# First modulation sums in halves of c, a first pass over two k tiles, `uhi` of the first tiles on ScalarE, and later gate-weight loads

## The chip, the cores and the metric

The kernel runs on one core of one Trainium2 chip. A core has a matrix engine, TensorE (PE in the rows below, with PEld for its weight loads), and VectorE (DVE), ScalarE (ACT), GpSimd (POOL) and SyncE (SP), each with its own instruction queue that is worked in order; they meet at semaphores. The metric is the device time of one execution in microseconds, as the median of several runs.

## The reference

Two layers of a decoder trunk work on x (256 tokens by 1024 channels) under a conditioning vector c of 1024. Each layer has three sub-layers: a SwiGLU channel mixer, a sequence mixer (recurrent in layer 0, attention in layer 1) and another channel mixer. All are modulated by c:

```python
c_act = jax.nn.silu(c)
for l in range(DEPTH):
    mod = c_act @ mod_w[l] + mod_b[l]
    sh1, sc1, g1, sh2, sc2, g2, sh3, sc3, g3 = jnp.split(mod, N_MOD, axis=-1)
    f = swiglu(modulate(x, sh1, sc1), ffn_in[l, 0], ffn_out[l, 0])
    x = deepnorm_residual(x, f, g1, ln_g[l, 0], ln_b[l, 0], 0.5)
    ...
```

`modulate(x, shift, scale)` is `x * (1 + scale) + shift`, and `swiglu(u, w_in, w_out)` is `(silu(u @ gate half) * (u @ up half)) @ w_out` with a hidden width of 2816, 22 tiles of 128. What matters here is the very first channel mixer: its input u needs shift and scale, and each of their 1024 values is a sum over 1024 products of c with a row of `mod_w`.

## The kernel before

**Layout.** Channels lie on the 128 partitions, in KD = 8 tiles, and the 256 tokens on the free axis. All weights are cut into tiles of 128x128 and stored in the order of their use; 16 tiles make a slab of 1 MB, `wst[s]`, and 170 slabs make up the whole plan. A second list of 72 slabs, `modw`, holds the modulation weights: each has two rows-of-`mod_w` tiles of 128x1024, in the first eight slabs the shift and the scale of one k tile.

**Precision.** A product is made of three matmuls (`mm3`, L413 to L422): the weights are split into `whi` (ACT, a rounding copy, L348) and `wlo` (DVE, the rest, L349), and u into `uhi` and `ulo`; hi times hi, lo times hi and hi times lo are added in PSUM. A slab is converted in two halves of 1024 columns, so it takes two `whi`, two `wlo` and 48 matmuls. Only slab 0 (k = 0 of the first pass) is taken as it came, with plain float32 matmuls (L417).

**Streams.** The class `Stream` (L303 on) issues the loads on SyncE, into a pool of six buffers `wraw` that weight slabs and modulation slabs share; `FIRST_MODS` (L227) says how many modulation slabs are to be asked for by each of the first twelve weight slabs, and the first eight also bring one tile of x with them (L388). `conv_to` converts slabs some halves ahead of their use. `reduce` (L392 to L401) makes one value per partition of a modulation tile: one DVE instruction that multiplies with `cact`, the activated c on every partition, sums, and starts from the bias column `mod_b`; a short read of the accumulator follows it.

**The first channel mixer.** The pairs of gate and up tiles are worked in passes, each over a group of eight pairs that fill the eight PSUM banks:

```python
a, b = range(GRP), range(GRP, 2 * GRP)
return [(a, range(KSPLIT)), (b, range(KD)), (a, range(KSPLIT, KD))]
```

With KSPLIT = 4, group a is taken over k = 0 to 3, its partial sums are copied out of PSUM by ACT (L761), group b runs over all eight k, and group a ends over k = 4 to 7, where the copies are added (L767). One k of one group is exactly one slab. Before a slab that uses a new k, `first_u(k)` (L515 to L533) makes u for it: two sums, `scp` = 1 + scale on DVE (L525), `ut` on ACT (L527), `uhi` on DVE (L531), `ulo` = `ut` - `uhi` on DVE (L532), and ax = ALPHA times x on ACT (L539).

**What sets the order.** The framework's scheduler lays the instructions out on each engine's queue, by the order in which the code asks for them and by priorities (`tc.high_priority`); `queue_behind` ties one instruction behind another without a semaphore. In the recurrent mixer of layer 0, each of eight gate-weight tiles `rgt` is loaded by a DMA that ACT issues (L865); three buffers are free from the start, so the first three issues stand at the head of ACT's queue. `shift_out` (L587 on) copies the first output tile of a sub-layer in ACT (L593) for a matmul with ones, whose result is subtracted from ax on POOL.

**The start.** c arrives, two matmuls with a row of ones spread it over the partitions (L453), ACT applies SiLU in two halves (`cact`, L442), and twelve matmuls with no use for their result (L459) follow on PE ahead of the first slab.

Of the kernel before, what the change touches and what calls it, by code (L numbers as in the profile page):

```python
# [21 lines left out]
P = 128  # L22
DM = 1024
# [8 lines left out]
NMOD = 9  # L32
# [3 lines left out]
MH, NOPE, ROPE, MV = 8, 128, 64, 128  # L36
QR, KVR = 256, 128
SLAB = 16
GRP = 8
KSPLIT = 4  # L40
GRPE = 4
EARLY = 1

# [180 lines left out]
    return out  # L224


FIRST_MODS = (1, 2, 3, 4, 4, 4, 5, 5, 6, 7, 8, 8)  # L227
SHARE = (13, 11, 18, 18, 0, 4)
SKIP = (12, 14, 6, 6, 3, 8)
ENDGAP = 1  # L230
# [4 lines left out]
def trunk_kernel(ctx: ExitStack, tc: tile.TileContext, xT, cvec, pos, wst, modw, colsd,  # L235
# [24 lines left out]
    def T(pl, shape, dt=F32, tag=None, **kw):  # L260
        return pl.tile(shape, dt, tag=tag, name=nm(tag), **kw)
# [41 lines left out]
    class Stream:  # L303
# [74 lines left out]
        def mods_to(self, n):  # L378
            while self.nmod < n:
                t = T(wraw, [P, 2, DM], tag="wraw")  # L380
                if self.nmod:
                    sync.dma_start(t, modw[self.nmod])
                else:
                    sync.dma_start(t[:, 0, :], modw[0, :, 0])
                    sync.dma_start(cols, colsd)
                    sync.dma_start(t[:, 1, :], modw[0, :, 1])
                if self.nmod < KD:
                    sync.dma_start(x0[:, self.nmod, :], xT[:, self.nmod, :])  # L388
                self.todo += [(2 * self.nmod + q, t[:, q, :], self.ndma) for q in range(2)]
                self.nmod += 1  # L390

        def reduce(self):  # L392
            i, t, _ = self.todo.pop(0)
            l, v, j = MODS[i]
            if (l, v) not in self.modcols:
                self.modcols[(l, v)] = T(const, [P, KD], tag=f"mod{l}_{v}")
            junk = T(wk, [P, DM], BF16, tag="junk", bufs=1)
            i = vec.tensor_tensor_reduce(junk, t, cact, 1.0, col("mod_b", (l * NMOD + v) * KD + j),  # L398
                                         MULT, ADD, self.modcols[(l, v)][:, j:j + 1])
            if self.behind is not None:  # L400
                queue_behind(i, self.behind)  # L401
# [48 lines left out]

    for i in range(2):
        ps = mmps()
        pe.matmul(ps, one_row, crow[:, i * 512:(i + 1) * 512], start=True, stop=True)  # L453
        ta(cact[:, i * 512:(i + 1) * 512], ps, AF.Silu)


    ps = mmps()
# [50 lines left out]
        ta(cosT, n, AF.Sin, scale=-1.0, bias=hp)  # L508


    scp0 = T(const, [P, KD], tag="scp0")
    W.dma_to(1)
    first_done = set()

    def first_u(k):  # L515
        if k in first_done:
            return
        first_done.add(k)

        W.mods_to(k + 1)  # L520
        while W.todo and W.todo[0][0] < 2 * k + 2:
            W.reduce()
        kk = slice(k, k + 1)
        sc0, sh0 = W.modcols[(0, SC)], W.modcols[(0, SH)]
        vec.tensor_scalar(scp0[:, kk], sc0[:, kk], 1.0, None, ADD)  # L525
        ut = T(wk, [P, SEQ], tag="ut")
        act.activation(ut, x0[:, k, :], AF.Identity, bias=sh0[:, kk], scale=scp0[:, kk])  # L527
        if k < RAWSLABS:
            u_raw[k] = ut
        else:  # L530
            vec.tensor_scalar(uhi[:, k, :], x0[:, k, :], scp0[:, kk], sh0[:, kk], MULT, ADD)  # L531
# [10 lines left out]
    class Boundary:  # L542
# [44 lines left out]
        def shift_out(self):  # L587


            y = self.y[:, 0, :]  # L590
            yr = T(wk, [P, SEQ], F32R, tag="shift", bufs=1)
            with tc.high_priority():
                act.activation(yr, y, AF.Copy)  # L593
            sp = axps()
            pe.matmul(sp[:, :SEQ], ones_r, yr, start=True, stop=True)
            shift = T(wk, [P, SEQ], tag="shift", bufs=1)
            with tc.high_priority():
                act.activation(shift, sp[:, :SEQ], AF.Copy)  # L598
                for j in range(1, KD):
                    pool.tensor_tensor(ax[:, j, :], ax[:, j, :], shift, SUB)  # L600
                vec.tensor_tensor(y, y, shift, SUB)
                ysq = T(wk, [P, SEQ], tag="ysq")
                act.activation(ysq, y, AF.Square)
                self.scaled(0)
            self.p0 = (y, ysq)
# [220 lines left out]
    def even(l, prev):  # L826
        with tc.tile_pool(name=nm("even"), bufs=1) as ep, tc.tile_pool(name=nm("ew"), bufs=2) as ew:
# [28 lines left out]
            def rglru(j0):  # L856
                rg1 = T(ep, [P, 2, RB, SEQ], tag="ya1")
                rg2 = T(ep, [P, 2, RB, SEQ], tag="ya2")
                xc, tz, pz, ww = rg1[:, 0], rg1[:, 1], rg2[:, 0], rg2[:, 1]
                for q in range(RB):  # L860
                    j = j0 + q
                    kk = slice(j, j + 1)
                    x = xc[:, q, :]
                    rgt = T(ew, [P, 2, P], tag="rgt", bufs=3)
                    act.dma_start(rgt, rgw[j])  # L865
                    act.activation(x, xa[:, j, hw:], AF.Identity, bias=col("conv_b", j),
                                   scale=col("conv_w", hw * KD + j))
# [484 lines left out]
```

## Time and profile before

| what | value |
|---|---|
| runs | 1031.18, 1032.38 and 1034.73 us; median 1032.38 |
| profiled execution | 1033.28 us, of which the span from the first instruction to the last is 1031.5 us |
| granted TensorE clock, mean | 0.992 |
| weights and the rest read from HBM | 256.18 MB, 249 GB/s over the span |
| `whi`, ACT, 128x1024 | 338 of 1056 ns |
| `wlo`, DVE, 128x1024 | 338 of 1228 ns |
| modulation sum, DVE, 128x1024 | 144 of 1294 ns |

The profile is one execution, recorded by the hardware. A row of the view in order of time gives the start, the length (both in us), the engine, the line, the operation, what it writes and reads, and in brackets how long the engine stood idle before it and what ended that. "x2" joins two equal instructions that follow each other; the next one can start a little before the end of the last, so two `wlo` of 1.23 take 2.36. A busy PE is not PE at its peak, since matmuls overlap: two that follow each other start 0.11 apart and are shown with 0.28 each.

### The profile page before, as it was taken

Reading aid. Unit: us, or ns where it says so; the run is one execution under the profiler, and the core shown is the slowest. Engines: PE = TensorE matmul, PEld = TensorE weight load, DVE = VectorE, ACT = ScalarE, POOL = GpSimd, SP = SyncE. Lnnn points to the kernel's source line nnn. Section 1 sums busy time; section 2 is a strip of 40 time slices with the busy share of each in tenths; the row PEclk is TensorE's granted clock in tenths of the full one; section 3 lists DMA queues with packets and bytes.
Section 4 is the critical chain, followed back from the end, with each engine's and each line's share of the span. In section 5 each row is a group of like instructions: output and inputs, shape, how many; then the busy total and the mean of one; then the engine's idle time right before and its main releaser. Section 6 shows DMA issues by size and latency. Waiting matters only on the chain.

```text
span 1031.5 us, 20651 instructions
## 1 busy us (share of the span) xinstructions
PE 1001.4 (97%) x8346; PEld 978.3 (95%) x8346; DVE 887.0 (86%) x1498; ACT 606.2 (59%) x1014; POOL 54.7 (5%) x70
## 2 busy tenths in 40 slices
PE   8999999999999989999999999999999999999995
PEld 6999999998989979999999999999999889999995
DVE  5889999798999789999897899999888799666664
ACT  3646664678886656645545674454568666545442
POOL 0000011000000020000030000003000200000200
PEclk9999999999999999999999999999999999999998
DMA  9998798655566924799976479987743236666411
GB/s 345 415 349 323 272 347 313 232 203 193 196 247 258 346 98 170 261 377 377 363 290 251 165 261 371 344 330 324 286 164 123 83 127 255 237 240 244 166 41 41
DMA packets 38578, 258.57 MB, mean 251 GB/s; under 512 B 4289, under 2 KB 6849, under 8 KB 7762
## 3 DMA queue, kind: packets, MB, share of 16 engines
q1 hardware_dynamic: 37330, 256.20, 66.3%
q8 instruction: 65, 1.06, 0.4%
q10 hardware_dynamic: 1152, 1.05, 0.3%
q14 instruction: 31, 0.25, 0.1%
HBM read 256.18 MB, written 1.05 MB: 249 GB/s over the span
## 4 chain that ended last, share of the span: by engine, by line
PE 82%; DVE 11%; ACT 3%; issue 2%; DMA 2%; POOL 0%; SPq 0%; ACTq 0%; DVEq 0%
PE mm L420 25%; PE mm L422 25%; PE mm L421 25%; DVE wlo L349 3%; DVE junk L398 2%; DMA rgt<-rgw 1%; DMA wraw<-modw 1%; PE mm L1022 1%; PE mm L1021 1%; PE mm L1023 1%; ACT whi L348 1%; PE ax L422 1%; PE ax L421 1%; PE ax L420 1%; DVE acc L618 0%
## 5 line engine op out<-in xcount | busy, mean ns | idle before, releaser
L349 DVE TENSOR_TENSOR wlo<-wraw,whi 128x1024 fp32r<-128x1024 f32 x338 | 412.1, 1228 | 76.4 <-ACT whi L348 75.5
L420 PE MATMUL mm<-uhi,whi 128*128 128x256 f32 x1660 | 458.3, 278 | 7.9 <-ACT whi L348 3.6
L421 PE MATMUL mm<-ulo,whi 128*128 128x256 f32 x1660 | 458.7, 277 | 0.5 <-DVE ulo L463 0.5
L422 PE MATMUL mm<-uhi,wlo 128*128 128x256 f32 x1660 | 456.4, 277 | 0.5 <-DVE wlo L349 0.5
L348 ACT ACTIVATE whi<-wraw 128x1024 fp32r<-128x1024 f32 x338 | 353.6, 1056 | 171.9 <-PE mm L421 139.0
L420 PEld LDWEIGHTS mm<-uhi,whi 128*128 128x128 f32 x1660 | 311.3, 188 | 9.9 <-ACT whi L348 4.4
L421 PEld LDWEIGHTS mm<-ulo,whi 128*128 128x128 f32 x1660 | 312.3, 188 | 1.0 <-DVE ulo L463 0.7
L422 PEld LDWEIGHTS mm<-uhi,wlo 128*128 128x128 f32 x1660 | 311.5, 188 | 0.8 <-DVE wlo L349 0.7
L422 PE MATMUL mm<-hhi,wlo 128*128 128x256 f32 x704 | 194.5, 276 | 0.8 <-DVE wlo L349 0.8
L421 PE MATMUL mm<-hlo,whi 128*128 128x256 f32 x704 | 194.3, 276 | 0.0
L420 PE MATMUL mm<-hhi,whi 128*128 128x256 f32 x704 | 194.3, 276 | 0.0
L398 DVE CUSTOM_DVE_ANT_0 junk<-wraw,cact,cols 128x1024 bf16<-128x1024 f32 x144 | 186.4, 1294 | 7.3 <-DMA wraw<-modw 6.7
L422 PEld LDWEIGHTS mm<-hhi,wlo 128*128 128x128 f32 x704 | 132.2, 188 | 1.0 <-DVE wlo L349 1.0
L420 PEld LDWEIGHTS mm<-hhi,whi 128*128 128x128 f32 x704 | 132.2, 188 | 0.0
L421 PEld LDWEIGHTS mm<-hlo,whi 128*128 128x128 f32 x704 | 132.2, 188 | 0.0
L600 POOL TENSOR_TENSOR ax<-ax,shift 128x256 f32<-128x256 f32 x42 | 47.9, 1173 | 840.8 <-ACT shift L598 667.2
L462 ACT ACTIVATE hhi<-h 128x256 fp32r<-128x256 f32 x88 | 35.7, 413 | 61.2 <-DVE h L731 60.9
L614 ACT ACTIVATE ysq<-yy 128x256 f32<-128x256 f32 x42 | 17.4, 414 | 60.8 <-DVE yy L610 58.8
L610 DVE SCALAR_TENSOR_TENSOR yy<-mm,gate,ax 128x256 f32<-128x256 f32 x48 | 22.9, 478 | 17.7 <-PE mm L422 16.5
L731 DVE SCALAR_TENSOR_TENSOR h<-mm,sg 128x256 f32<-128x256 f32 x75 | 30.8, 416 | 8.1 <-PE mm L422 8.1
L463 DVE TENSOR_TENSOR hlo<-h,hhi 128x256 fp32r<-128x256 f32 x88 | 35.8, 415 | 0.0
L442 ACT ACTIVATE sg<-mm 128x256 f32<-128x256 f32 x75 | 27.5, 367 | 4.2 <-PE mm L422 3.0
(296 smaller groups left out, 1103.4 us busy)
## 6 DMA issues: line engine op xcount, KB each, us to landing
wraw<-wst SPq DMA_DIRECT2D x169, 1024.0 KB, 5.2
wraw<-modw SPq DMA_DIRECT2D x71, 1024.0 KB, 7.1
wraw<-modw SPq DMA_DIRECT2D x2, 512.0 KB, 5.3
rgt<-rgw ACTq DMA_DIRECT2D x8, 128.0 KB, 4.6
yy<-xT SPq DMA_DIRECT2D x8, 128.0 KB, 9.2
wraw<-wst SPq DMA_DIRECT2D x2, 512.0 KB, 6.4
outT<-yy SPq DMA_DIRECT2D x3, 256.0 KB, 2.7
outT<-yy SPq DMA_DIRECT2D x2, 128.0 KB, 2.7
```

The lines of the kernel that those rows point to most:

```text
L348: act.activation(hi, raw, AF.Copy)
L349: i = vec.tensor_tensor(lo, raw, hi.bitcast(F32), SUB)
L398: i = vec.tensor_tensor_reduce(junk, t, cact, 1.0, col("mod_b", (l * NMOD + v) * KD + j), MULT, ADD, self.modcols[(l, v)][:, j:j + 1])
L420: pe.matmul(ps, hi, mh, start=start, stop=False, skip_group_check=shared)
L421: pe.matmul(ps, hi, ml, start=False, stop=False, skip_group_check=shared)
L422: pe.matmul(ps, lo, mh, start=False, stop=stop, skip_group_check=shared)
L442: i = act.activation(out, in_, func, **kw)
L462: act.activation(hi, src, AF.Copy)
L463: return vec.tensor_tensor(lo, src, hi.bitcast(F32), SUB)
L600: pool.tensor_tensor(ax[:, j, :], ax[:, j, :], shift, SUB)
L610: vec.scalar_tensor_tensor(y, ps, self.gate[:, f:f + 1], ax[:, f, :], MULT, ADD)
L731: vec.scalar_tensor_tensor(h, pu, bu, sg, ADD, MULT)
```

## The change

It has four parts.

1. The first modulation slab is loaded in two halves of c (columns 0 to 511 of both tiles, then the rest), not tile by tile. The first two sums are made in halves: `modh` takes the first half's sum, with the bias, and the second half starts from it. The 1 + of the scale moves into the bias column `scb`, made once, so `scp` is gone for all eight k.
2. KSPLIT is 2, so the first pass is over k = 0 and 1, group b runs over eight k as before, and group a ends over k = 2 to 7. `FIRST_MODS` follows: slabs 0 and 1 bring a modulation slab each, slab 2 none, slabs 3 to 8 one each.
3. `uhi` of k = 1 to 7 is made on ACT, ahead of `ut`.
4. The first three loads of `rgt` are queued behind the copy in the first `shift_out` (`mark`).

```diff
-KSPLIT = 4
+CH = DM // 2
+KSPLIT = 2
...
-FIRST_MODS = (1, 2, 3, 4, 4, 4, 5, 5, 6, 7, 8, 8)
+FIRST_MODS = (1, 2, 2, 3, 4, 5, 6, 7, 8, 8, 8, 8)
...
-                    sync.dma_start(t[:, 0, :], modw[0, :, 0])
+                    sync.dma_start(t[:, :, :CH], modw[0, :, :, :CH])
                     sync.dma_start(cols, colsd)
-                    sync.dma_start(t[:, 1, :], modw[0, :, 1])
+                    sync.dma_start(t[:, :, CH:], modw[0, :, :, CH:])
...
-            i = vec.tensor_tensor_reduce(junk, t, cact, 1.0, col("mod_b", (l * NMOD + v) * KD + j),
+            if i < 2:
+                if i == 0:
+                    for q in range(2):
+                        tq = self.first[:, q, :CH]
+                        lq, vq, jq = MODS[q]
+                        vec.tensor_tensor_reduce(junk[:, :CH], tq, cact[:, :CH], 1.0,
+                                                 mod_init(lq, vq, jq), MULT, ADD, modh[:, q:q + 1])
+                vec.tensor_tensor_reduce(junk[:, CH:], t[:, CH:], cact[:, CH:], 1.0, modh[:, i:i + 1],
+                                         MULT, ADD, self.modcols[(l, v)][:, j:j + 1])
+                return
+            i = vec.tensor_tensor_reduce(junk, t, cact, 1.0, mod_init(l, v, j),
...
+    def mod_init(l, v, j):
+        return scb[:, j:j + 1] if (l, v) == (0, SC) else col("mod_b", (l * NMOD + v) * KD + j)
...
+    vec.tensor_scalar(scb, col("mod_b", SC * KD, KD), 1.0, None, ADD)
...
-        sc0, sh0 = W.modcols[(0, SC)], W.modcols[(0, SH)]
-        vec.tensor_scalar(scp0[:, kk], sc0[:, kk], 1.0, None, ADD)
+        scp0, sh0 = W.modcols[(0, SC)], W.modcols[(0, SH)]
+        if k >= RAWSLABS:
+            act.activation(uhi[:, k, :], x0[:, k, :], AF.Identity, bias=sh0[:, kk], scale=scp0[:, kk])
         ut = T(wk, [P, SEQ], tag="ut")
         act.activation(ut, x0[:, k, :], AF.Identity, bias=sh0[:, kk], scale=scp0[:, kk])
...
-            vec.tensor_scalar(uhi[:, k, :], x0[:, k, :], scp0[:, kk], sh0[:, kk], MULT, ADD)
...
-                act.activation(yr, y, AF.Copy)
+                self.mark = act.activation(yr, y, AF.Copy)
...
-                    act.dma_start(rgt, rgw[j])
+                    i = act.dma_start(rgt, rgw[j])
+                    if j < 3:
+                        queue_behind(i, prev.mark)
```

The order of the instructions shows where this leads. On ACT, the first pass and what follows it stood before like this, from the `ut` of k = 2 to the first copy of a partial sum (names end in a buffer's number; `wraw` is a slab as loaded, `yy` holds x):

```order
L527 ACTIVATE ut_310<-yy_115,mod_0_41_167,scp_23_141 128x256
L348 ACTIVATE whi_213<-wraw_184 128x1024
L348 ACTIVATE whi_227<-wraw_184 128x1024
L539 ACTIVATE ax_138<-yy_115 128x256
L527 ACTIVATE ut_374<-yy_115,mod_0_41_167,scp_23_141 128x256
L348 ACTIVATE whi_249<-wraw_189 128x1024
L348 ACTIVATE whi_279<-wraw_189 128x1024
L761 ACTIVATE flat_88_440<-mm_159 128x512
L348 ACTIVATE whi_317<-wraw_191 128x1024
L348 ACTIVATE whi_345<-wraw_191 128x1024
```

After the change, ACT has from the copies of the last partial sums to the slab that follows k = 3:

```order
L783 ACTIVATE flat_76_311<-ax_168 128x512
L561 ACTIVATE ax_140<-yy_115 128x256
L548 ACTIVATE uhi_138<-yy_115,mod_0_42_169,mod_1_44_174 128x256
L550 ACTIVATE ut_459<-yy_115,mod_0_42_169,mod_1_44_174 128x256
L349 ACTIVATE whi_250<-wraw_189 128x1024
L349 ACTIVATE whi_282<-wraw_189 128x1024
L561 ACTIVATE ax_140<-yy_115 128x256
L548 ACTIVATE uhi_138<-yy_115,mod_0_42_169,mod_1_44_174 128x256
L550 ACTIVATE ut_526<-yy_115,mod_0_42_169,mod_1_44_174 128x256
L349 ACTIVATE whi_333<-wraw_194 128x1024
L349 ACTIVATE whi_365<-wraw_194 128x1024
```

The `uhi` and `ut` of k = 2 now stand ahead of the `whi` of slab 3, those of k = 3 ahead of slab 4, and so on; with k = 7 alone the two `whi` stand between `uhi` and `ut`.

On DVE, before, one k ended and the next slabs' `wlo` followed, with no sums between them for three slabs (`junk` is a sum's unused product; the row behind it reads the accumulator):

```order
L525 TENSOR_SCALAR scp_23_141<-mod_1_43_170 128x1
L531 TENSOR_SCALAR uhi_136<-yy_115,scp_23_141,mod_0_41_167 128x256
L532 TENSOR_TENSOR ulo_137<-ut_374,uhi_136 128x256
L349 TENSOR_TENSOR wlo_250<-wraw_189,whi_249 128x1024
L349 TENSOR_TENSOR wlo_280<-wraw_189,whi_279 128x1024
L349 TENSOR_TENSOR wlo_318<-wraw_191,whi_317 128x1024
L349 TENSOR_TENSOR wlo_346<-wraw_191,whi_345 128x1024
L349 TENSOR_TENSOR wlo_385<-wraw_207,whi_384 128x1024
L349 TENSOR_TENSOR wlo_413<-wraw_207,whi_412 128x1024
L398 ISA junk_467,mod_0_41_167<-wraw_244,cact_96,cols_97 128x1024
```

Now DVE has, from the second `wlo` of slab 2 on:

```order
L350 TENSOR_TENSOR wlo_231<-wraw_184,whi_230 128x1024
L413 ISA junk_254,mod_0_42_169<-wraw_186,cact_96,cols_97 128x1024
L413 ISA mod_0_42_169 128x1
L413 ISA junk_256,mod_1_44_174<-wraw_186,cact_96,scb_117 128x1024
L413 ISA mod_1_44_174 128x1
L554 TENSOR_TENSOR ulo_139<-ut_459,uhi_138 128x256
L350 TENSOR_TENSOR wlo_251<-wraw_189,whi_250 128x1024
L350 TENSOR_TENSOR wlo_283<-wraw_189,whi_282 128x1024
L413 ISA junk_337,mod_0_42_169<-wraw_191,cact_96,cols_97 128x1024
L413 ISA mod_0_42_169 128x1
L413 ISA junk_339,mod_1_44_174<-wraw_191,cact_96,scb_117 128x1024
L413 ISA mod_1_44_174 128x1
```

The same group of two sums, `ulo` and two `wlo` comes six times in a row, for k = 2 to 7 and slabs 3 to 8.

The third place is ACT around the first `shift_out`, where the copy of `yy` (L593 before) was followed by a `whi` and the copy of the shift; now three DMA issues stand between:

```order
L615 ACTIVATE shift_1965<-yy_1794 128x256
L887 DMA rgt_3143<-rgw 128x256
L887 DMA rgt_3159<-rgw 128x256
L887 DMA rgt_3175<-rgw 128x256
L349 ACTIVATE whi_1955<-wraw_1694 128x1024
L620 ACTIVATE shift_1969<-ax_1967 128x256
```

These are the three issues that stood ahead of everything but a table load and one copy at the head of ACT's queue.

More of the change, by code (lines that the diff above doesn't have):

```diff
@@ L383, in mods_to @@
                 else:
-                    sync.dma_start(t[:, 0, :], modw[0, :, 0])
+                    sync.dma_start(t[:, :, :CH], modw[0, :, :, :CH])
                     sync.dma_start(cols, colsd)
-                    sync.dma_start(t[:, 1, :], modw[0, :, 1])
+                    sync.dma_start(t[:, :, CH:], modw[0, :, :, CH:])
                 if self.nmod < KD:
                     sync.dma_start(x0[:, self.nmod, :], xT[:, self.nmod, :])
+                if self.nmod == 0:
+                    self.first = t
                 self.todo += [(2 * self.nmod + q, t[:, q, :], self.ndma) for q in range(2)]
@@ L410, in trunk_kernel @@
     x0 = T(main, [P, KD, SEQ], tag="yy")
+    modh = T(const, [P, 2], tag="modh")
+    scb = T(const, [P, KD], tag="scb")
+    def mod_init(l, v, j):
+        return scb[:, j:j + 1] if (l, v) == (0, SC) else col("mod_b", (l * NMOD + v) * KD + j)
     W = Stream()
@@ L452, in trunk_kernel @@
         ps = mmps()
-        pe.matmul(ps, one_row, crow[:, i * 512:(i + 1) * 512], start=True, stop=True)
-        ta(cact[:, i * 512:(i + 1) * 512], ps, AF.Silu)
+        pe.matmul(ps, one_row, crow[:, i * CH:(i + 1) * CH], start=True, stop=True)
+        ta(cact[:, i * CH:(i + 1) * CH], ps, AF.Silu)
     ps = mmps()
@@ L508, in rope_tables @@
         ta(cosT, n, AF.Sin, scale=-1.0, bias=hp)
-    scp0 = T(const, [P, KD], tag="scp0")
     W.dma_to(1)
+    vec.tensor_scalar(scb, col("mod_b", SC * KD, KD), 1.0, None, ADD)
     first_done = set()
```

## The prediction

> **What bounds the kernel now.** I read the page first, then the busy time by stretch, then who waited for whom on TensorE, then the three engines' instructions in order of time up to 70 us.
>
> ```profile
> span 1031.5 us, 20651 instructions
> PE 1001.4 (97%) x8346; PEld 978.3 (95%) x8346; DVE 887.0 (86%) x1498; ACT 606.2 (59%) x1014; POOL 54.7 (5%) x70
> PE mm L420 <- ACT whi L348: 3.6, 3, 1.6
> 19.40:26.16 6.76, 5.77 (x48) 5.57 (x48) 5.85 (x10) 2.91 (x5) 0.00 (x0) 1.00 1.02 418
> 26.16:32.91 6.75, 5.77 (x48) 5.57 (x48) 5.84 (x10) 2.80 (x5) 0.00 (x0) 1.00 1.01 421
> 64.90:124.00 59.10, 58.64 (x518) 58.44 (x516) 58.02 (x97) 37.14 (x63) 0.00 (x0) 1.00 0.78 292
> 124.00:163.30 39.30, 38.52 (x337) 38.32 (x337) 39.30 (x66) 20.02 (x27) 8.98 (x7) 1.00 0.89 340
> ```
>
> TensorE (PE) is busy for 97% of the span: a saving anywhere else counts only where it shortens a wait of PE. The changed instructions stand in the first 160 us, so I look for PE's waits there. The third row (wait, total, times, longest) gives three waits for `whi` between 10 and 70 us. The stretches (length, then busy time of PE, PEld, DVE, ACT, POOL, granted clock, DMA share, GB/s) show a slab of 48 matmuls taking 6.76 us twice, and VectorE (DVE) nearly full from 65 to 163 us. PE's own rows, in order of time:
>
> ```profile
> 6.03 4.37 PE L459 MATMUL mm<-ones_dm,ident 128*128 128x128 f32 x24
> 10.63 5.45 PE L417 MATMUL mm<-ut,wraw 128*128 128x256 f32 x24 [0.23 <-ACT ut L527]
> 19.41 0.38 PE L420 MATMUL mm<-uhi,whi 128*128 128x256 f32 x1 [1.60 <-ACT whi L348]
> 24.90 0.28 PE L422 MATMUL ax<-uhi,wlo 128*128 128x256 f32 x1
> 26.17 0.38 PE L420 MATMUL mm<-uhi,whi 128*128 128x256 f32 x1 [0.99 <-ACT whi L348]
> 32.92 0.38 PE L420 MATMUL mm<-uhi,whi 128*128 128x256 f32 x1 [0.99 <-ACT whi L348]
> 38.56 0.28 PE L420 MATMUL mm<-uhi,whi 128*128 128x256 f32 x1
> 66.03 0.28 PE L420 MATMUL mm<-uhi,whi 128*128 128x256 f32 x1
> 124.03 0.38 PE L422 MATMUL mm<-uhi,wlo 128*128 128x256 f32 x1 [0.49 <-DVE wlo L349]
> 163.40 0.38 PE L422 MATMUL mm<-hhi,wlo 128*128 128x256 f32 x1 [0.85 <-DVE wlo L349]
> ```
>
> I number slabs by the order of the plan: slab 0 is the raw one (L417), slab 1 starts at 19.41, slab 4 at 38.56 and slab 9 at 66.03. From 38.56 on PE does not wait for long: (66.03 - 38.56) / 5 = 5.49 us a slab. Slab 1, which starts cold, ends at 24.90 + 0.11, so 5.60 from its start. After that PE waits only twice, 0.49 and 0.85, both for DVE's `wlo`.
>
> **Why slabs 2 and 3 cost 6.76.** This is one turn, on DVE and then ACT:
>
> ```profile
> 24.20 0.08 DVE L398 DVE_READ_ACCUMULATOR2_ANT mod<- 128x1 f32 x1
> 24.31 0.15 DVE L525 TENSOR_SCALAR scp<-mod 128x1 f32<-128x1 f32 x1
> 24.50 0.41 DVE L531 TENSOR_SCALAR uhi<-yy,scp,mod 128x256 fp32r<-128x256 f32 x1
> 26.15 2.36 DVE L349 TENSOR_TENSOR wlo<-wraw,whi 128x1024 fp32r<-128x1024 f32 x2 [0.52 <-ACT whi L348]
> 28.42 1.28 DVE L398 CUSTOM_DVE_ANT_0 junk<-wraw,cact,cols 128x1024 bf16<-128x1024 f32 x1
> 30.96 0.08 DVE L398 DVE_READ_ACCUMULATOR2_ANT mod<- 128x1 f32 x1
> 24.57 0.60 ACT L527 ACTIVATE ut<-yy,mod,scp 128x256 f32<-128x256 f32 x1 [3.41 <-DVE scp L525]
> 25.07 1.99 ACT L348 ACTIVATE whi<-wraw 128x1024 fp32r<-128x1024 f32 x2
> ```
>
> The sums end at 24.28 (24.20 + 0.08). `ut` starts 0.29 later, `whi` 0.50 after that, `wlo` 1.08 after `whi`, the next two sums 2.27 after `wlo`, and they last 2.62 (28.42 to 31.04): 6.76. Nothing in this turn overlaps, because each conversion of a slab stands behind the next k's sums on DVE and behind its `ut` on ACT. PE starts a slab 1.10 after its first `whi` (25.07 to 26.17). The turn is longer than a slab's 5.49, so PE waits. Before, only three slabs in a row pay it; slabs 4 to 7 need no sums, and their conversions run ahead of PE.
>
> **What the change does to the turn.** It takes `scp` and the DVE `uhi` out, and puts `uhi` on ACT ahead of `ut`, both now in front of `whi`. From the sums' end: 0.11 to ACT's `uhi` (scp's end 24.46 to `ut` 24.57 is the same handover), 0.50 to `ut`, 0.50 to `whi`, then 1.08, 2.27 and 2.62 as before: **7.08**. The new `uhi` is the same function, inputs and size as `ut`, so I take its pitch; less than 0.33 (a plain 128x256 activation's) or more than 0.60 would surprise me, so 6.91 to 7.18. DVE has 0.56 less work a step and waits instead. And with two k tiles in the first pass, the sums for k = 2 to 7 are asked for in six slabs one after the other (slabs 3 to 8), with no slabs free of sums between.
>
> **The start.** Splitting the first sums lets two quarters run ahead, but two still follow the second transfer:
>
> ```profile
> 8.46 1.28 DVE L398 CUSTOM_DVE_ANT_0 junk<-wraw,cact,cols 128x1024 bf16<-128x1024 f32 x1 [0.25 <-DMA wraw<-modw]
> 9.98 0.60 ACT L527 ACTIVATE ut<-yy,mod,scp 128x256 f32<-128x256 f32 x1 [0.73 <-DVE scp L525]
> 14.96 1.29 DVE L398 CUSTOM_DVE_ANT_0 junk<-wraw,cact,cols 128x1024 bf16<-128x1024 f32 x1 [5.02 <-DMA wraw<-modw]
> q1 hardware_dynamic: 1611, 6.10, 82.4%
> q10 hardware_dynamic: 432, 0.39, 6.1%
> ```
>
> Halves save no work behind the landing, only `scp`. It would hardly matter: PE runs its warm-up matmuls (L459) until 10.40 in any case, and waits 0.23 for `ut`. That 0.23 is all that the first slab can gain: it starts at 10.40 and ends at 17.6.
>
> What does move is the second modulation tile, since three gate-weight loads leave the queue ahead of it. In the first 20 us they take 6.1% of the DMA engines (q10), 1.22 us. Against that stand shorter rows in the first tile: 1 MB at q10's 0.39 MB in 1.22 us instead of q1's 6.10 MB in 16.5 us would cost 0.4 us more at worst, nothing at best. So the landing comes 0.8 to 1.2 earlier; I take 1.0, and the k = 1 sums start at 13.96. The Trainium skill (DMA: Bandwidth & Descriptors, Issuing engines are not separate DMA queues) says that transfers started by ScalarE run on the same 16 DMA engines and interleave with SyncE's. The trace agrees as far as it can: both queues' shares in the first 20 us add to 88.5% while the sums wait 5.02. Were the queues separate, this 1.0 would not come, and the forecast below would be 1.0 higher.
>
> **The sum.** k = 1 sums end at 13.96 + 2.62 = 16.58; `uhi` 16.69, `ut` 17.19, `whi` 17.69; PE starts slab 1 at 18.79 (was 19.41) and slab 2 at 24.39.
>
> ```profile
> 35.01 0.60 ACT L761 ACTIVATE flat<-mm 128x512 f32<-128x512 f32 x1 [1.19 <-PE mm L422]
> 35.50 2.00 ACT L348 ACTIVATE whi<-wraw 128x1024 fp32r<-128x1024 f32 x2
> ```
>
> At the end of the first pass a partial sum's copy stands ahead of the next `whi`, as before at 35.01, 2.09 after its slab's start; `whi` follows 0.49 later. Now: copy 20.88, `whi` 21.37, `wlo` 22.46, k = 2 sums 24.73 to 27.35, `whi` 28.46, `wlo` 29.54. Slab 3 could start at 29.88 but needs the first `wlo` (30.7) for its third matmul: 0.7 lost, and not on the path, since the turn sets what follows. k = 3 sums 31.81 to 34.43, `whi` 35.54, so slab 4 starts at 36.64; slabs 5, 6 and 7 at steps of 7.08: 43.72, 50.80, 57.88. Slab 8's `whi` stands ahead of `ut`, 0.50 less: 64.46. Slab 9 starts 5.60 later, at 70.06, against 66.03: **+4.0 us**.
>
> DVE is by then no later than before. At 64.5 it has slabs 8 and 9 still to convert, 2 x 2.27, plus `ulo` 0.34: 69.3, where before it began slab 10 at
>
> ```profile
> 69.09 4.63 DVE L349 TENSOR_TENSOR wlo<-wraw,whi 128x1024 fp32r<-128x1024 f32 x4 [0.53 <-ACT whi L348]
> ```
>
> PE reaches 124 and 163 us 4.0 later with DVE on time, so its waits of 0.49 and 0.85 go: -1.3. Copies, gate and later modulation sums are the same in number; DVE's full stretch covers them. The moved gate loads put three DMA issues on ACT, at 0.43 each as at the start, behind the copy of `yy`:
>
> ```profile
> 147.30 0.42 ACT L593 ACTIVATE shift<-yy 128x256 fp32r<-128x256 f32 x1 [0.38 <-DVE yy L610]
> 148.56 1.06 ACT L348 ACTIVATE whi<-wraw 128x1024 fp32r<-128x1024 f32 x1 [0.84 <-PE mm L421]
> 154.25 0.42 ACT L603 ACTIVATE ysq<-yy 128x256 f32<-128x256 f32 x1 [4.36 <-DVE yy L601]
> ```
>
> 1.3 us of issue meet 0.84 idle there and 4.36 soon after; queued behind them are a `whi` and the shift's copy. I take 0; without that idle it is 0.5 to 1.3. In all +4.0 - 1.3 = **+2.7**. The profiled execution, 1033.28 with a span of 1031.5, would become 1036.0; the median of the runs, 1032.38, becomes 1035.1.
>
> **Rivals.**
> - *The late start carries through*: PE waits elsewhere in place of 124 and 163 (for the copy of `yy` behind the three issues, say). +4.0 or more: 1036.4 and up. For it: DVE's 100%; against: its place in time computed above. 0.13.
> - *DVE hides it*: DVE sets PE's pace until 163, not only at two points, and PE's lateness is mostly absorbed: 0 to +1, about 1032.9. For it: 58.02 of 59.10 busy; against: only 1.34 of PE waiting there. 0.15.
> - *Faster*: the turn does not bind, because sums run ahead of conversions. Then slab 9 starts at 24.39 + 7 x 5.49 = 62.8, 3.2 early: 1029.2. It decides at a turn under 5.49; the rows say 7.08, and the order of the instructions leaves no room. 0.09.
> - *A lower granted clock* from six broken slabs. Each turn would have 1.5 us of idle in 7.1:
>
> ```profile
> 225.00:250.00 25.00, 25.00 (x122) 20.26 (x121) 20.90 (x32) 20.39 (x33) 0.00 (x0) 1.00 0.47 166
> ```
>
> Half the usual matmuls there, and the clock (1.00) stays. At half clock in slabs 3 to 8 (6 x 5.5 us doubled, less the idle) it would be 20 us more: 1055. 0.03. The Trainium skill (TensorE: Matmul & The Clock Gate, HAM oscillation) puts the fall of the clock at idle gaps above about 3.4 us; by that rule, too, gaps of 1.5 do nothing.
>
> **How the numbers follow.** Forecast 0.60, 1033.4 to 1036.7 by the turn's bounds (six times -0.17 to +0.10), the landing (0.2) and the 0 to 1.3. A measurement tells about 0.3% (3.1 us) from no change: the forecast's own range gives 0.36 within that and 0.24 slower. With the rivals: slower 0.24 + 0.13 + 0.03 = 0.40; the same 0.36 + 0.15 + half of the faster case = 0.55; faster 0.05. The range reaches from 1031.8 to 1037.4: it leaves out the faster case, the clock and thin ends.
>
> **What would show it.** Right: sums from k = 2 to 7 follow each other at 7.0 to 7.2, PE waits for `whi` at slabs 4 to 8 with about 1.5 in the middle ones, slab 9 starts near 70, and no `wlo` waits remain near 127 and 166. Wrong: sums of k = 3 before the `wlo` of slab 3; a first raw matmul before 10.3; slab 9 before 67; or a new wait of PE between 120 and 170.

## The result, and the profile after

Over 22 runs each, the kernel before has a median of 1032.11 us (1030.66 to 1037.12) and the changed one 1035.32 us (1033.74 to 1039.28). The ratio is 1.003, 95% interval 1.0019 to 1.004: the change costs 3.2 us, or 2.0 to 4.1 by the interval. The forecast was 1035.1. The profiled execution took 1036.01 us, with a span of 1034.3. One execution of a kernel below, passes_only, took 3578.41 us where its other eleven took 1033.49 to 1038.85; its median and ratio are those of the eleven.

The first lines of the changed kernel's page, and from its view of waits the row of PE's waits for `whi` (us in total, times, longest):

```profile
span 1034.3 us, 20643 instructions
PE 1002.2 (97%) x8346; PEld 978.9 (95%) x8346; DVE 883.8 (85%) x1488; ACT 609.9 (59%) x1021; POOL 53.9 (5%) x70
PE mm L441 <- ACT whi L349: 5.1, 6, 1.2
```

Before, the same row had three waits with 3.6 us in total; now there are six with 5.1. Averages hide this: no engine's share moved by more than a point. The six waits, and five other points of PE's work, in order of time:

```profile
11.37 0.59 PE L438 MATMUL mm<-ut,wraw 128*128 128x256 f32 x1
19.18 0.39 PE L441 MATMUL mm<-uhi,whi 128*128 128x256 f32 x1 [0.53 <-ACT whi L349]
24.80 0.28 PE L441 MATMUL mm<-uhi,whi 128*128 128x256 f32 x1
31.13 0.39 PE L443 MATMUL mm<-uhi,wlo 128*128 128x256 f32 x1 [0.50 <-DVE wlo L350]
36.87 0.39 PE L441 MATMUL mm<-uhi,whi 128*128 128x256 f32 x1 [0.22 <-ACT whi L349]
43.87 0.39 PE L441 MATMUL mm<-uhi,whi 128*128 128x256 f32 x1 [1.21 <-ACT whi L349]
50.87 0.38 PE L441 MATMUL mm<-uhi,whi 128*128 128x256 f32 x1 [1.24 <-ACT whi L349]
57.87 0.38 PE L441 MATMUL mm<-uhi,whi 128*128 128x256 f32 x1 [1.20 <-ACT whi L349]
64.38 0.39 PE L441 MATMUL mm<-uhi,whi 128*128 128x256 f32 x1 [0.75 <-ACT whi L349]
69.98 0.28 PE L441 MATMUL mm<-uhi,whi 128*128 128x256 f32 x1
166.71 0.39 PE L443 MATMUL mm<-hhi,wlo 128*128 128x256 f32 x1 [0.99 <-DVE wlo L350]
```

The first row is slab 0, then come slabs 1 and 2, a stall inside slab 3, slabs 4, 5, 6, 7, 8 and 9, and the wait for `wlo` that stood at 163.40 before. From slab 4 to slab 7 they stand exactly 7.00 apart, and slab 9 starts 3.95 later than before (66.03). One turn on DVE, then the ACT instructions between its two halves:

```profile
39.12 1.28 DVE L413 CUSTOM_DVE_ANT_0 junk<-wraw,cact,cols 128x1024 bf16<-128x1024 f32 x1
40.45 1.28 DVE L413 CUSTOM_DVE_ANT_0 junk<-wraw,cact,scb 128x1024 bf16<-128x1024 f32 x1
41.66 0.08 DVE L413 DVE_READ_ACCUMULATOR2_ANT mod<- 128x1 f32 x1
43.85 2.36 DVE L350 TENSOR_TENSOR wlo<-wraw,whi 128x1024 fp32r<-128x1024 f32 x2 [0.52 <-ACT whi L349]
46.13 1.28 DVE L413 CUSTOM_DVE_ANT_0 junk<-wraw,cact,cols 128x1024 bf16<-128x1024 f32 x1
41.78 0.60 ACT L548 ACTIVATE uhi<-yy,mod,mod 128x256 fp32r<-128x256 f32 x1 [3.71 <-DVE mod L413]
42.28 0.59 ACT L550 ACTIVATE ut<-yy,mod,mod 128x256 f32<-128x256 f32 x1
42.78 1.99 ACT L349 ACTIVATE whi<-wraw 128x1024 fp32r<-128x1024 f32 x2
```

From sum to sum it is 46.13 - 39.12 = 7.01. ACT stands idle for 3.71 of it, waiting for a sum, with a `whi` queued behind that needs nothing from the sum. That is the loss in one row.

### The profile page after: what moved, and what is told of

The parts are those of the page before. It is cut to its first block, busy times and chain, and to the rows that moved or that the text cites. A ratio compares the mean times of both kernels' runs of the same rounds, so it can differ in the third digit from the quotient of the medians.

```text
span 1034.3 us, 20643 instructions
## 1 busy us (share of the span) xinstructions
PE 1002.2 (97%) x8346; PEld 978.9 (95%) x8346; DVE 883.8 (85%) x1488; ACT 609.9 (59%) x1021; POOL 53.9 (5%) x70
## 4 chain that ended last, share of the span: by engine, by line
PE 81%; DVE 10%; ACT 3%; issue 3%; DMA 2%; SPq 0%; POOL 0%; DVEq 0%; ACTq 0%
PE mm L441 25%; PE mm L442 24%; PE mm L443 24%; DVE wlo L350 3%; DVE junk L413 2%; ACT whi L349 1%; DMA wraw<-modw 1%; DMA rgt<-rgw 1%; PE mm L1046 1%; PE mm L1045 1%; PE mm L1047 1%; ACT ya L463 0%; DVE acc L640 0%; DVE yy L632 0%; DVE acc L639 0%
## 5 line engine op out<-in xcount | busy, mean ns | idle before, releaser
L413 DVE CUSTOM_DVE_ANT_0 junk<-wraw,cact,cols 128x1024 bf16<-128x1024 f32 x135 | 175.3, 1299 | 6.5 <-DMA wraw<-modw 6.2
```

The lines of the kernel that those rows point to most:

```text
L413: i = vec.tensor_tensor_reduce(junk, t, cact, 1.0, mod_init(l, v, j), MULT, ADD, self.modcols[(l, v)][:, j:j + 1])
```

## The experiments

Each kernel was run beside the kernel before, in four batches in which the kernel before had medians of 1032.11, 1032.27, 1033.1 and 1032.17. The ratio is taken within a batch, so medians of different rows are not to be subtracted to the tenth. Traces are one execution each. The table puts them together: from the traces the start of slabs 1, 4 and 9 and of the first matmul with gate weights (`ax<-ya,rgt`), all in us, and from the runs the ratio to the kernel before. The gate matmul is the first point after all work that the change touches, and before the places where the granted clock of single executions differs (last section).

| kernel | slab 1 | slab 4 | slab 9 | gate | gate, against before | median | ratio, 95% interval |
|---|---|---|---|---|---|---|---|
| before | 19.41 | 38.56 | 66.03 | 252.84 | 0 | 1032.11 | 1 |
| changed | 19.18 | 36.87 | 69.98 | 256.14 | +3.30 | 1035.32 | 1.003, 1.0019 to 1.004 |
| uhi_on_dve | 18.62 | 35.50 | 67.28 | 253.38 | +0.54 | 1032.6 | 1.0002, 0.9987 to 1.0018 |
| passes_only | 19.00 | 36.12 | 68.78 | 255.33 | +2.49 | 1035.54 | 1.0027, 1.0011 to 1.0043 |
| old_passes | 19.62 | 39.24 | 66.87 | 254.01 | +1.17 | 1033.29 | 1.0005, 0.9988 to 1.0023 |
| part_1_only | 18.86 | 37.64 | 65.10 | 251.94 | -0.90 | 1031.68 | 1.0002, 0.9988 to 1.0017 |
| late_gate_loads_only | 18.19 | 37.33 | 64.77 | 251.64 | -1.20 | 1030.8 | 0.9992, 0.9977 to 1.0008 |
| old_passes_short_turn | 18.65 | 37.42 | 64.92 | 251.94 | -0.90 | 1032.03 | 0.9989, 0.997 to 1.0008 |
| convert_first | 19.05 | 35.58 | 62.77 | 248.96 | -3.88 | 1028.3 | 0.9957, 0.9941 to 0.9973 |
| before_convert_first | 19.16 | 35.65 | 62.85 | 249.45 | -3.39 | 1029.24 | 0.997, 0.9959 to 0.9981 |
| convert_first_early_gate | 19.47 | 35.94 | 63.14 | 249.72 | -3.12 | 1029.82 | 0.9973, 0.9959 to 0.9986 |
| convert_first_whole | 18.78 | 35.27 | 62.47 | 248.95 | -3.89 | 1028.29 | 0.9965, 0.9947 to 0.9983 |

### uhi_on_dve

```diff
-        if k >= RAWSLABS:
-            act.activation(uhi[:, k, :], x0[:, k, :], AF.Identity, bias=sh0[:, kk], scale=scp0[:, kk])
...
+            vec.tensor_scalar(uhi[:, k, :], x0[:, k, :], scp0[:, kk], sh0[:, kk], MULT, ADD)
```

> The changed kernel with uhi of k = 1 to 7 back on DVE; the rest of the change stays, so the result is the reference's. Theory (a turn of DVE sums, ACT, DVE wlo sets PE's slabs 3 to 8, and the activation of uhi stands in it): the turn falls from 7.00 to 6.50 us, slab 1 and each of slabs 3 to 8 come 0.50 earlier, slab 9 starts near 67.0 (69.98 in the changed kernel, 66.03 before), and the time is near 1032.5, 1031.5 to 1033.2. Rival (DVE's load sets the pace until 163 us, so 7 x 0.33 us more of work on DVE costs more than ACT saves): sums still about 7 us apart or the gain lost again by 163 us, time 1035 or more.

PE's slabs 5, 6 and 7 of this kernel:

```profile
41.97 0.39 PE L441 MATMUL mm<-uhi,whi 128*128 128x256 f32 x1 [0.49 <-ACT whi L349]
48.54 0.38 PE L441 MATMUL mm<-uhi,whi 128*128 128x256 f32 x1 [0.78 <-ACT whi L349]
55.11 0.39 PE L441 MATMUL mm<-uhi,whi 128*128 128x256 f32 x1 [0.81 <-ACT whi L349]
```

The turn is 6.57, slab 9 starts at 67.28 and the median is 1032.6, where 6.50, 67.0 and 1032.5 were expected. The rival falls: DVE takes seven more instructions and the kernel is 2.7 us faster than the changed one. In these passes the place of `uhi` alone is worth 256.14 - 253.38 = 2.76 us at the gate matmul, and the two intervals of the ratio do not overlap.

### passes_only and old_passes

Part 2 alone, on the kernel before (old_passes is the reverse of this diff, on the changed kernel):

```diff
-KSPLIT = 4
+KSPLIT = 2
-FIRST_MODS = (1, 2, 3, 4, 4, 4, 5, 5, 6, 7, 8, 8)
+FIRST_MODS = (1, 2, 2, 3, 4, 5, 6, 7, 8, 8, 8, 8)
```

> The kernel before with part 2 of the change alone (first pass over two k tiles, and the list of modulation slabs that goes with it). Theory: six turns of the old 6.76 us in a row; slab 1 at 19.4, slab 8 near 63.6, slab 9 near 69.2 (66.03 before), and DVE gives back some 0.7 by 170 us: time near 1034.5, 1033.8 to 1035.2. Rival (the place of uhi, not the passes, is what cost the time): slab 9 within 1 us of 66.03 and the time within 0.7 of the kernel before, near 1032.

> The changed kernel with the first pass over four k tiles again and the old list of modulation slabs: parts 1, 3 and 4 of the change without part 2. Theory: two turns of 7.00 after a start that is 0.23 earlier: slab 2 at 26.2, slab 3 at 33.2, slab 4 at 38.8 (38.56 before), time near 1032.4, 1031.6 to 1033.2. Rival (the halved first sums, uhi on ACT or the later gate loads carry the loss by themselves): slab 4 later than 40, or a new wait between 70 and 170 us, time 1034 or more.

Slabs 6 and 7 of passes_only, and slabs 2 and 3 of old_passes:

```profile
49.63 0.38 PE L420 MATMUL mm<-uhi,whi 128*128 128x256 f32 x1 [0.98 <-ACT whi L348]
56.39 0.39 PE L420 MATMUL mm<-uhi,whi 128*128 128x256 f32 x1 [0.98 <-ACT whi L348]
...
26.62 0.38 PE L441 MATMUL mm<-uhi,whi 128*128 128x256 f32 x1 [1.20 <-ACT whi L349]
33.62 0.39 PE L441 MATMUL mm<-uhi,whi 128*128 128x256 f32 x1 [1.23 <-ACT whi L349]
```

With the new passes alone the turn is the old 6.76 (56.39 - 49.63), but six k in a row need it; with the old passes it is the new 7.00 (33.62 - 26.62), but only two k do. Slab 9 of passes_only starts at 68.78 (expected 69.2), slab 4 of old_passes at 39.24 (expected 38.8; its slab 1 was 0.4 later than expected, for a landing, below). Both the length of the turn and how often it is taken carry the loss. Both medians lie above the ranges expected, 1035.54 against 1033.8 to 1035.2 and 1033.29 against 1031.6 to 1033.2. Passes_only's interval, 1.1 to 4.4 us, holds the trace's 2.49; old_passes cannot be told from the kernel before by its interval.

### part_1_only, late_gate_loads_only and old_passes_short_turn

The kernel before with one or two pieces of the change's diff. part_1_only has the halves and the new bias column, cut to its core:

```diff
-                    sync.dma_start(t[:, 0, :], modw[0, :, 0])
+                    sync.dma_start(t[:, :, :CH], modw[0, :, :, :CH])
...
-                    sync.dma_start(t[:, 1, :], modw[0, :, 1])
+                    sync.dma_start(t[:, :, CH:], modw[0, :, :, CH:])
...
+    vec.tensor_scalar(scb, col("mod_b", SC * KD, KD), 1.0, None, ADD)
...
-        vec.tensor_scalar(scp0[:, kk], sc0[:, kk], 1.0, None, ADD)
```

late_gate_loads_only has the gate loads:

```diff
-                act.activation(yr, y, AF.Copy)
+                self.mark = act.activation(yr, y, AF.Copy)
...
-                    act.dma_start(rgt, rgw[j])
+                    i = act.dma_start(rgt, rgw[j])
+                    if j < 3:
+                        queue_behind(i, prev.mark)
```

old_passes_short_turn has this second diff and the last two lines of the first (`scb` in place of `scp`), with whole tiles and sums. `uhi` stays on DVE in all three.

> The kernel before with part 1 alone: first modulation tile in halves of c, first sums in halves, the 1 + of the scale in the bias column. Theory of the forecast (the halves save nothing behind the landing and cost the start at most 0.4 us of DMA time; scp's absence shortens the turn): sums of k = 1 start near 15.0 (14.36 to 14.94 with the gate loads there so far), slab 1 near 19.3, then two turns of 6.57, slab 4 near 38.0 (38.56 before), time 0.2 to 0.8 below the kernel before. Rival (halves make a late start: raw slab at 11.4 and slab 1 later than 19.8): slab 4 at 38.6 or later, time the same or more.

> The kernel before with part 4 alone (the first three gate loads queued behind the first shift copy). Theory of the forecast (the three loads take 1.2 us of DMA time ahead of the second modulation tile, and it lands 1.0 earlier without them): the sums of k = 1 start near 13.6, slab 1 near 18.4 (19.41 before), and the time is 0.3 to 1.0 below the kernel before. Rival (the landing depends on other things: with the loads it was 14.94 in the kernel before and 14.36 in passes_only, without them 14.30, 14.23, 14.74 and 14.17): the sums start between 14.1 and 15.0, slab 1 between 18.6 and 19.5, the time within 0.4 of the kernel before.

> The kernel before with the 1 + of the scale in the bias column (scp gone) and the later gate loads; uhi on DVE, whole tiles and the first pass over four k as before. Theory (the turn, here twice): 6.57 as in uhi_on_dve, so slab 1 near 18.7, slab 2 25.3, slab 3 31.9, slab 4 37.5 (38.56 before), and 1.0 of that stays to the end: time near 1031.2, 1030.5 to 1032. Rival (DVE sets PE's pace until 163 us, so an earlier start is only waited off): the waits for wlo near 124 and 163 grow by 1 us together and the time is within 0.4 of the kernel before.

The first sum of k = 1, which waits for the second modulation tile, in late_gate_loads_only, old_passes_short_turn, convert_first_whole (whole tiles, no gate loads ahead), then in part_1_only and convert_first_early_gate (halves, gate loads ahead) and the changed kernel's sibling old_passes (halves, none ahead):

```profile
13.74 1.28 DVE L398 CUSTOM_DVE_ANT_0 junk<-wraw,cact,cols 128x1024 bf16<-128x1024 f32 x1 [4.16 <-DMA wraw<-modw]
...
14.39 1.28 DVE L402 CUSTOM_DVE_ANT_0 junk<-wraw,cact,cols 128x1024 bf16<-128x1024 f32 x1 [4.76 <-DMA wraw<-modw]
...
14.03 1.28 DVE L403 CUSTOM_DVE_ANT_0 junk<-wraw,cact,cols 128x1024 bf16<-128x1024 f32 x1 [4.54 <-DMA wraw<-modw]
...
14.60 1.28 DVE L413 CUSTOM_DVE_ANT_0 junk<-wraw,cact,cols 128x1024 bf16<-128x1024 f32 x1 [4.10 <-DMA wraw<-modw]
...
14.72 1.28 DVE L414 CUSTOM_DVE_ANT_0 junk<-wraw,cact,cols 128x1024 bf16<-128x1024 f32 x1 [4.19 <-DMA wraw<-modw]
...
14.88 1.28 DVE L413 CUSTOM_DVE_ANT_0 junk<-wraw,cact,cols 128x1024 bf16<-128x1024 f32 x1 [4.11 <-DMA wraw<-modw]
```

One profile of each is not enough for this: the same four edits at the start gave 14.43 in the changed kernel, 14.36 in uhi_on_dve, 14.30 in convert_first and 14.88 in old_passes, a spread of 0.58. Means do better. Whole tiles with the gate loads start the sums at 14.96, 14.38 and 14.51 (before, passes_only, before_convert_first), mean 14.62; without them at 13.74, 14.39 and 14.03, mean 14.05. Halves give 14.66 with the loads and 14.49 without. So the later gate loads seem to bring some 0.6 where the first tile comes whole, and the halves to take most of that back (14.49 against 14.05). With two to four profiles each and a spread of 0.58, neither is firmly shown.

The three kernels of this section reach slab 4 earlier than before, by 0.92, 1.23 and 1.14, and 0.9 to 1.2 is still there at the gate matmul. Their turn is 6.57 in part_1_only (32.00 - 25.43, slabs 2 and 3) and in old_passes_short_turn (31.80 - 25.23), as in uhi_on_dve. The rival on waits is not borne out by the traces, but these gains of about 1 us are inside every interval of the ratio. The time that part_1_only was to gain, 0.2 to 0.8, does not show in its ratio of 1.0002.

### convert_first

The same instructions as in the changed kernel, in another order. `whi_of` and `wlo_of` keep the conversions by half slab; 2k + 3 is the second half of slab k + 1.

```diff
-                act.activation(hi, raw, AF.Copy)
-                i = vec.tensor_tensor(lo, raw, hi.bitcast(F32), SUB)
+                self.whi_of[s] = act.activation(hi, raw, AF.Copy)
+                i = self.wlo_of[s] = vec.tensor_tensor(lo, raw, hi.bitcast(F32), SUB)
...
-            act.activation(uhi[:, k, :], x0[:, k, :], AF.Identity, bias=sh0[:, kk], scale=scp0[:, kk])
+            i = act.activation(uhi[:, k, :], x0[:, k, :], AF.Identity, bias=sh0[:, kk], scale=scp0[:, kk])
+            if k >= 2:
+                queue_behind(i, W.whi_of[2 * k + 3])
...
-        act.activation(ut, x0[:, k, :], AF.Identity, bias=sh0[:, kk], scale=scp0[:, kk])
+        i = act.activation(ut, x0[:, k, :], AF.Identity, bias=sh0[:, kk], scale=scp0[:, kk])
+        if k >= 2:
+            queue_behind(i, W.whi_of[2 * k + 3])
...
             u_last[0] = vec.tensor_tensor(ulo[:, k, :], ut, uhi[:, k, :].bitcast(F32), SUB)
+            if k >= 2:
+                queue_behind(u_last[0], W.wlo_of[2 * k + 3])
```

> The changed kernel with the same instructions in another order for k = 2 to 7: uhi and ut on ACT are queued behind both whi of the slab that they held up, and ulo on DVE behind both wlo of it. Theory (the turn is a matter of order: whi needs nothing of the sums that it stands behind): DVE's work for one k is 2.62 + 0.34 + 2.27 = 5.23 us, less than PE's 5.49 a slab, so PE runs from slab 1 on without waiting, slab 9 starts near 63.2 (69.98 in the changed kernel, 66.03 before), and the time falls below both kernels, near 1029, 1026 to 1030.5. First rival (DVE's load until 163 us is the bound, the order is not): PE's lead is lost in new waits for wlo before 170 us, time 1032 or more. Second rival (the landing of the slabs sets the pace, the DMA engines being 99% busy from 10 to 60 us): PE waits for whi and that waits for DMA, slabs 3 to 8 more than 6 us apart.

Its PE at slabs 1, 2 and 9; a turn on DVE; and ACT beside it:

```profile
19.05 0.39 PE L442 MATMUL mm<-uhi,whi 128*128 128x256 f32 x1 [1.58 <-ACT whi L350]
24.70 0.28 PE L442 MATMUL mm<-uhi,whi 128*128 128x256 f32 x1
62.77 0.28 PE L442 MATMUL mm<-uhi,whi 128*128 128x256 f32 x1
...
40.65 1.27 DVE L414 CUSTOM_DVE_ANT_0 junk<-wraw,cact,cols 128x1024 bf16<-128x1024 f32 x1
41.86 0.41 DVE L559 TENSOR_TENSOR ulo<-ut,uhi 128x256 fp32r<-128x256 f32 x1
42.19 1.27 DVE L414 CUSTOM_DVE_ANT_0 junk<-wraw,cact,scb 128x1024 bf16<-128x1024 f32 x1
43.40 2.35 DVE L351 TENSOR_TENSOR wlo<-wraw,whi 128x1024 fp32r<-128x1024 f32 x2
45.67 1.27 DVE L414 CUSTOM_DVE_ANT_0 junk<-wraw,cact,cols 128x1024 bf16<-128x1024 f32 x1
...
42.08 2.01 ACT L350 ACTIVATE whi<-wraw 128x1024 fp32r<-128x1024 f32 x2 [2.13 <-DMA wraw<-wst]
43.99 0.59 ACT L549 ACTIVATE uhi<-yy,mod,mod 128x256 fp32r<-128x256 f32 x1
```

DVE's turn is 45.67 - 40.65 = 5.02 without a gap (5.23 expected), and PE goes from slab 1 to slab 9 without a wait: (62.77 - 24.70) / 7 = 5.44 a slab. Now `whi` waits for the landing of its slab, but runs ahead of PE: slab 6 starts at 46.45 on PE. The `whi` at 42.08 is that slab's. The median of 1028.3 is 3.8 us below the kernel before and 7.0 below the changed one; the traces have 7.18 between the two at the gate matmul. The instructions are the changed kernel's own, so the first rival (DVE's work sets the time) falls, and the second (the DMA) with it.

### before_convert_first, convert_first_early_gate and convert_first_whole

before_convert_first is the kernel before with the new passes and this order, without parts 1, 3 and 4; on DVE `uhi` goes behind `wlo` as well:

```diff
+            i = vec.tensor_scalar(uhi[:, k, :], x0[:, k, :], scp0[:, kk], sh0[:, kk], MULT, ADD)
+            if k >= 2:
+                queue_behind(i, W.wlo_of[2 * k + 3])
```

convert_first_early_gate is convert_first without part 4:

```diff
-                    i = act.dma_start(rgt, rgw[j])
-                    if j < 3:
-                        queue_behind(i, prev.mark)
+                    act.dma_start(rgt, rgw[j])
```

convert_first_whole is convert_first with the first modulation tile loaded and summed whole:

```diff
-                    sync.dma_start(t[:, :, :CH], modw[0, :, :, :CH])
+                    sync.dma_start(t[:, 0, :], modw[0, :, 0])
...
-                    sync.dma_start(t[:, :, CH:], modw[0, :, :, CH:])
+                    sync.dma_start(t[:, 1, :], modw[0, :, 1])
```

> The kernel before with the first pass over two k tiles and with the conversions of a slab ahead of ut (ACT), uhi and ulo (DVE) of k = 2 to 7; none of the parts 1, 3 and 4, so scp and uhi stay on DVE. Theory: DVE's work for one k is 2.62 + 0.08 + 0.33 + 0.34 + 2.27 = 5.64 us, near PE's 5.49, so PE waits at most 0.2 a slab; slab 1 near 19.2, slab 9 near 63.5 to 64.2, time near 1029, 1028 to 1030.3. Rival (the gain of convert_first comes from uhi on ACT, the halved sums or the later gate loads): slab 9 later than 65.5, time 1031 or more.

> convert_first without part 4: the three gate loads are at the head of ACT's queue again. Theory of the forecast: the second modulation tile lands 1.0 later (15.2 against 14.17), slab 1 starts near 20.0 and all that follows is 1.0 later: time near 1029.3. Rival (its landing does not depend on these loads): sums of k = 1 start between 14.1 and 15.0, time within 0.5 of convert_first's 1028.3.

> convert_first with the first modulation tile loaded and summed whole again, as before (scb, uhi on ACT, the passes and the later gate loads stay). Theory (the halves give nothing, and cost the landing of the second tile some 0.3: without gate loads it was 13.71 and 14.26 in whole tiles, 14.30, 14.23, 14.74 and 14.17 in halves): slab 1 near 18.7, slab 9 near 62.4 (62.77 in convert_first), time 1027.5 to 1028.5. Rival (the halves help the start, since two of the four sums run before the second half lands): slab 1 at 19.4 or later, time 1028.8 or more.

Passes and order alone give 3.39 of the 3.88 us at the gate matmul; the three other parts bring 0.5 together, or nothing that the ratios can tell. Slab 9 of before_convert_first came at 62.85, ahead of the 63.5 to 64.2 expected. The early gate loads cost 0.76 at the gate matmul, between the two theories (sums of k = 1 at 14.72, neither 15.2 nor the same); the two ratio intervals overlap. Only 0.37 of the 0.76 is there at slab 9. The rest comes at PE's one later wait for `wlo`, near 160 us: 1.41 against 1.00 in convert_first. The other two kernels with the new passes and the early loads wait 1.40 and 1.44 there, and the four with the later loads 0.97 to 1.28; why is open. This wait also makes up most of the 0.5 of the three other parts, since at slab 9 they differ by 0.08. No kernel has the new order with the first pass over four k, so whether the new passes add anything to the order is not tested. Whole tiles start slab 9 0.30 earlier, but it is waited off before the gate matmul, at 248.95 against 248.96, and the medians agree to 0.01. Halves of c show no gain here.

## Why the prediction came out, step by step

- **The turn and its six repeats** were right: 7.08 worked out, 7.01 measured, and slab 9 at 70.06 against 69.98. The experiments bear out both factors on their own: the length (7.00, 6.76 and 6.57 by where `uhi` and `scp` stand) and the number (two or six). The stall of slab 3 came too, with 0.50 for the 0.7 forecast. That the activation of `uhi` is on the path was a sum of rows; uhi_on_dve showed it. PE's rows show 1.2 us of idle in the middle waits where about 1.5 was forecast. The lateness is as forecast, 7.00 - 5.49 = 1.51 a slab: the idle that a row shows is some 0.3 less than what the wait costs.
- **The start of slab 0** was wrong: 10.40 forecast, 11.37 measured. The forecast had PE's warm-up matmuls end at 10.40 in any case, and they did not:

```profile
6.08 5.49 PE L480 MATMUL mm<-ones_dm,ident 128*128 128x128 f32 x24
10.63 0.60 ACT L550 ACTIVATE ut<-yy,mod,mod 128x256 f32<-128x256 f32 x1 [0.97 <-DVE mod L410]
```

  They took 5.49 us, against 4.37 before: after the first they all start 0.21 apart, while before the last ten start 0.11 apart. The trace's first record of a granted clock stands at 11.71 us here and at 9.05 before. PE comes to slab 0 without idle time. `ut` alone would have allowed it at about 11.28 (10.63 + 0.65, the step from `ut` to slab 0 before), since the first sums waited 0.93 for their second half. In uhi_on_dve `ut` ended at 10.67, and slab 0 still started at 11.38, behind the warm-up; in convert_first, with the same start, both were early and it started at 10.30. As forecast for any move there, it cost nothing: slab 1 still waited for `whi`.
- **The landing of the second modulation tile** was mis-sized: 1.0 earlier assumed, 0.53 measured in the pair of profiles (14.96 to 14.43), 0.13 between the means of whole tiles with the loads and halves without (14.62 and 14.49). The cost of the halves, bounded at 0 to 0.4, comes out at 0.44 between the means (14.49 and 14.05), within their scatter. Slab 1 was 0.39 later than forecast, and the turns, 0.07 shorter each than worked out, made up for it by slab 9.
- **The two waits for `wlo` that would go** were half right. DVE did begin slab 10 on time (69.24, forecast 69.3), and the wait at 124 went; the one near 163 stayed, at 166.71, and grew by 0.15. The prediction had "no `wlo` waits remain near 127 and 166" among its signs of being right, and half of that failed. Matmul by matmul, PE's lateness goes from 3.95 to 3.15 at the first place, and from 3.17 to 3.33 at the second. What failed is "DVE on time" behind 69. From 75 to 163 us, before, changed, then convert_first, the busy times by stretch, and the changed kernel's DVE rows with idle time:

```profile
75.00:163.00 88.00, 87.06 (x766) 86.66 (x764) 87.87 (x148) 51.09 (x83) 8.98 (x7) 1.00 0.83 314
...
75.00:163.00 88.00, 88.00 (x779) 88.00 (x778) 85.97 (x141) 48.92 (x76) 8.25 (x7) 1.00 0.82 313
...
75.00:163.00 88.00, 87.00 (x767) 86.80 (x766) 85.96 (x148) 48.30 (x71) 8.17 (x7) 1.00 0.84 324
...
95.64 1.22 DVE L350 TENSOR_TENSOR wlo<-wraw,whi 128x1024 fp32r<-128x1024 f32 x1 [0.39 <-ACT whi L349]
101.08 1.22 DVE L350 TENSOR_TENSOR wlo<-wraw,whi 128x1024 fp32r<-128x1024 f32 x1 [0.31 <-ACT whi L349]
103.50 0.69 DVE L789 TENSOR_TENSOR flat<-mm,flat 128x512 f32<-128x512 f32 x1 [1.19 <-PE mm L443]
```

  The third busy time is DVE's. It loses 0.39 + 0.31 + 1.19 = 1.89 us ahead of the first sum with a kept partial result. The same three waits stand in every kernel with the new passes (convert_first too, which runs ahead of the kernel before), and in none with the old. So they come from part 2 and not from being late: group a now ends over six k at a stretch, where DVE's queue waits in order, first for ACT's `whi` and then for PE's last product. That these 1.89 us are what kept the second wait alive is argued from the rows and not tested by itself. The forecast took DVE's punctuality at 69 us as good to 163. In sum PE was 3.30 late at the gate matmul where +2.7 was forecast.
- **ACT's three gate issues** behind the shift copy cost nothing that the trace shows: PE is busy for all of 88.00 us in the second row above.
- **The agreement to 0.2 us is partly luck.** The landing and the turn were off in opposite directions. The two waits were mis-sized: -1.3 forecast for both, 3.95 - 3.30 = 0.65 measured (the first gave 0.80 where its row said 0.49, the second gave nothing), which is the whole step from +2.7 to +3.30; the medians lie 3.21 apart. The forecast's own range, 1033.4 to 1036.7, does not come out of the terms named for it, which give 1033.9 to 1037.2 around 1035.1; the measured median lies in both. And the changed kernel's profile hit its forecast of 1036.0 by a chance of the clock (below).

## What to carry to other kernels

Look in an in-order queue for an instruction that needs nothing of what it stands behind: here ACT stood idle for 3.71 us in each turn in front of a conversion that could have run, and putting that conversion first took 7.0 us off the changed kernel with no work less. Work out a loop over two engines as one turn, from hand-over to hand-over, and ask how many times in a row it is taken; work put on the idle engine lengthens the turn if it is put in front of what the other one waits for. And before a wait is written off as absorbed, ask whether the absorbing engine has work to do all the way there, or waits in order for the late one.

## What was not expected of the hardware

**The granted clock falls in some executions and not in others.** In twelve profiled executions, one of each kernel, the clock fell to half for about 3.4 to 7 us near 385 us in seven, near 835 in four, near 302 in one, and at none of these in three. All twelve have an idle gap of PE of 1.91 to 1.98 us near 379 to 387 us. PE stands in front of the same wait in the kernel before and in uhi_on_dve; the rows are PE's next matmul and the two stretches around it, of the first and then of the second kernel:

```profile
383.00 0.38 PE L420 MATMUL mm<-uhi,whi 128*128 128x256 f32 x1 [1.93 <-DVE yy L610]
380.00:384.00 4.00, 2.07 (x18) 1.88 (x17) 4.00 (x12) 3.07 (x6) 0.00 (x0) 1.00 0.00 0
384.00:388.00 4.00, 4.00 (x23) 4.00 (x23) 3.15 (x5) 0.92 (x1) 0.00 (x0) 0.57 0.28 72
...
383.55 0.38 PE L441 MATMUL mm<-uhi,whi 128*128 128x256 f32 x1 [1.93 <-DVE yy L631]
380.00:384.00 4.00, 2.07 (x19) 1.87 (x17) 4.00 (x11) 3.22 (x7) 0.23 (x1) 1.00 0.00 0
384.00:388.00 4.00, 4.00 (x38) 4.00 (x37) 4.00 (x7) 1.76 (x4) 0.00 (x0) 1.00 0.19 55
```

The same 1.93 us of idle in a stretch where PE is half busy: the clock falls to 0.57 in the one, 23 matmuls in place of 38, and stays at 1.00 in the other. The Trainium skill (TensorE: Matmul & The Clock Gate, HAM oscillation) warns of idle gaps above about 3.4 us; here a shorter one goes with the fall at times, and what decides between the two is not shown. The waits for `whi` of up to 1.24 us in every 7 that the change makes did not bring it on, as forecast: the granted clock is 1.00 from 36 to 65 us. Such stretches also make single profiles hard to compare. The kernel before has one near 835 and the changed one has not, and PE's delay falls from 4.03 us at its 6600th matmul to 2.79 at its 6900th. So the spans differ by 2.8 us, and the medians by 3.2.
